# Where the context's expert gathers run: rates of the background queue and 64 gathers of v in a hybrid backbone kernel

## The chip, the core and the metric

The kernel runs on one core of a Trainium2 chip. The metric is the device time of one execution in microseconds (us). A core has five engines with queues of their own: PE (TensorE, matrix products), DVE (VectorE), ACT (ScalarE), POOL (GpSimd, which here only issues indirect DMAs, the gathers) and SP (SyncE, which issues the plain DMAs). PEld is the weight load of PE. Each queue runs in the order in which its instructions stand, and waits for others by semaphores.

## What is computed

Two layers over 512 latent tokens and 256 context tokens of width 1024. A layer has a mixer and an expert stage (PEER):

```
p = h @ w_in[l]                    # one projection feeds four branches and their gates
ml, state = mlstm(p, state)        # two directions, state carried from the context's scan
z = [ml, gmlp(p), conv(p), fnet(p)]
y = sum(sigmoid(p_gate[i]) * (z[i] @ w_branch[i]) for i in range(4))
x = x + mod[2] * (y @ w_out)
# PEER: 8 heads x 16 experts of 16384 for each token
s = einsum('nhpk,pek->nhpe', hb @ w_q, keys); e, g = top16(s)
a = gelu(einsum('nhkd,nd->nhk', u_tab[e], hb)) * g
x = x + mod[5] * einsum('nhk,nhkd->nd', a, v_tab[e])
```

The context goes through PEER in layer 0 alone, and its result is needed first in layer 1's mixer.

## The kernel before

All activations lie transposed, channels on partitions. Products in fp32 accuracy are made of three passes with a high and a low half of each operand: `wload` (L298 to L302) loads 512 KB of weights on SP's queue, ACT makes the high half `wh`, DVE the low half `wl`, and PE runs 24 matmuls (`mm3`, L312). The programs' helper then calls `tick(5.1)`.

For PEER the kernel treats tokens in two ways. Three blocks of 128 latent tokens are computed densely: all experts' products `s` are formed in 128 "s-blocks" (some, 76 in layer 0 and 80 in layer 1, beside the routing, the rest in `dense`), and multiplied by the routing weights (`weights_dense`, L1079 to L1112) and by v (`acc`, L1191). The fourth latent block and the 256 context tokens fetch their experts' rows instead: one gather is an indirect DMA of 128 rows, 512 KB (`rows`, L907). A block of 128 tokens needs 128 gathers of u and 128 of v. For the latents' block each u gather is consumed by one DVE instruction (L938) and each v gather by another (L956). For the context (`gather_ctx`) there are four halves of 64 tokens, with 64 gathers of u and 64 of v each: a u gather is consumed by one DVE instruction of 1024 columns (L1017), two v gathers, a pair, by four matmuls of PE with 32 columns of weights (L1051).

Buffers: the context's u gathers in layer 0's mixer use the tile `ug` (3 buffers), v gathers the tile `gat` (5 buffers, of which one holds the diagonal `dg` for 16 pairs). POOL's queue issues gathers in order, each as soon as its buffer is free.

The gathers are fed into the program by a queue, `rows_bg`: each `tick(us)` of the foreground adds `us * rate` to a credit, and each unit of credit lets one gather be written into the program (a scheduler may then still move instructions a little on each engine). So the rates set beside which work the gathers stand. In layer 0 the queue holds, in this order: u of half 0 (64), then v of half 0 and u of half 1 in turns (128), then u of half 2 (64). The deferred ones are `gens`: v of half 1 and v of half 2 go into the routing of the latents' PEER (`first` of `peer_lat`, at 0.6 credit each and a rate of 0.4), u and v of half 3 into layer 1's mixer. In the routing the gathers of u for the latents' block follow, once that of `first` is done, and what is then left of them goes into `dense`, spread evenly over its 128 steps.

The stages of layer 0 from there on: the context's routing (L1378, up to 584 us), the latents' mLSTM (L1386), `conv` (L1387), four merges with `gmlp` and `fnet` between them (L1393 to L1397), `w_out` (L1402), and the latents' PEER (L1406): norm, 16 steps of the query product (the q steps), the rest of the routing, `dense`. Layer 1 has the same stages of the latents' PEER, but with no context gathers in them.

Of the kernel before, what the change touches and what calls it, by code (L numbers as in the profile page):

```python
# [37 lines left out]
NEG = -1.0e30  # L38
NCAND = 50
STARTS = [0, 16, 24, 29, 33, 36, 38, 40]  # L40
RATE = 0.75
RATE_A = 1.0
ML_TICK = 8.0
P_RATE = 0.28
P0 = (0.4, 0.35, 76)
# [16 lines left out]
def build(nc, tc, I, out):  # L62
# [119 lines left out]
    rows_bg, s_bg, ada_bg, conv_bg = (Background() for _ in range(4))  # L182
# [1136 lines left out]
    with psum_pool(mm=3, sm=3, acc=2):  # L1319
        mod, mod2 = (mk(pl, [128, 48, 2], F32, "modT") for _ in range(2))  # L1320
        C = layer_consts(0)
        mp_cm, mp = open_pool("mp", "left")
        with spool("cxa", 1) as cxa:
            cx_cm, cx = open_pool("cx", "left")
            use_bufs(cx, cx, CTX)
            third = lambda l, g, m: ada_bg.add(ada(l, g, m, cxa, NADA, ("acc", "acc")), 8, 2.0)
            ag = [third(0, g, mod) for g in range(3)]
            ada_bg.finish(ag[0])
            mixer_consts(0, C, cm)
            use_bufs(cx, cx, CTX)  # L1330
            hc = norm_mod(xc, CTX, mod, 1, C["norm1_g"], 0)
            ada_bg.rate = ADA_RATE
            side[0] = "right"
            zc, state = mlstm(0, C, hc, CTX, None, True, True, "zm")
            side[0] = "left"
            def lat_norm():
                use_bufs(pb, cx, SEQ)
                x_first(mp)
                nc.gpsimd.dma_start(xd.rearrange("(k p) t -> p k t", p=128), xl[0])
                hl.extend(norm_mod(xl[0], SEQ, mod, 0, C["norm1_g"], 0))  # L1340
                use_bufs(cx, cx, CTX)

            hl = []
            ctx_merge(0, C, mod, xc, hc, lambda: zc, lat_norm, lambda: ada_bg.finish(ag[2]))
            cx_cm.__exit__(None, None, None)
            cx_cm, cx = open_pool("cx", "left")
            use_bufs(cx, cx, CTX)
            ada_bg.rate = ADA_RATE2
            for g in range(3):
                third(1, g, mod2)  # L1350
            hc = norm_mod(xc, CTX, mod, 1, C["norm2_g"], 3, True)
            nc.gpsimd.dma_start(xcd.rearrange("(k p) t -> p k t", p=128), xc)
            close_right(xc_cm)
            pg_cm, pg[0] = right_pool("pg")
            pu_cm, pu[0] = right_pool("pu")
            hnd = mk(pd, [3, 128, D], F32, "hnd", 1)
            ond = mk(pd, [4, 128, 512], F32, "ond", 1)
            gens = []

            def start(b, i12, gw):  # L1360
                ua, va, ub, vb = gather_ctx(0, hc, b, i12, gw, hnd, ond)
                if b == 0:
                    rows_bg.add(ua(), 64)
                    rows_bg.add(weave(va(), 64, ub(), 64), 128)
                    rows_bg.rate = RATE_A
                    gens.append(vb)
                else:
                    rows_bg.add(ua(), 64)
                    gens.extend([va, ub, vb])

            big = mk(mp, [128, 5136], F32, "x")
            proj = (big[:, 0:2048].rearrange("p (j t) -> p j t", j=4),
                    big[:, 2048:3088].rearrange("p (c h d) -> p c h d", c=4, h=4),
                    big[:, 3088:4112].rearrange("p (c d) -> p c d", c=4),
                    big[:, 4112:5136].rearrange("p (c d) -> p c d", c=4))
            s_bg.add(mlstm_steps(0, C, hl, SEQ, *proj), 13)
            s_bg.rate, s_rate[0] = 0.0, P_RATE
            routing(0, C, hc, CTX, None, start)  # L1378
            s_bg.finish()
            ada_bg.finish()  # L1380
            after[0] = None
            cx_cm.__exit__(None, None, None)
        rows_bg.rate = RATE
        use_bufs(pb, None, SEQ)
        cv_cm, cv = right_pool("cv")
        zl_, _ = mlstm(0, C, hl, SEQ, state, True, False, None, proj)  # L1386
        end = conv(0, C, hl, SEQ, cv)  # L1387
        mp_cm.__exit__(None, None, None)
        zq_cm, zpool[0] = open_pool("zq", "left")
        zl_ = mlstm_z(zl_, SEQ, "zm")  # L1390
        with spool("ym", 1) as ym:
            y = mk(ym, [128, KT, SEQ], F32, "y")
            merge_one(0, 0, True, y, zl_, hl, SEQ)  # L1393
            for i in (1, 3):
                with spool("zb", 1) as zpool[0]:
                    merge_one(0, i, False, y, branch(i, 0, C, hl, SEQ), hl, SEQ)
            merge_one(0, 2, False, y, end(), hl, SEQ)  # L1397
            close_right(cv_cm)
            yp = y_parts(y, SEQ)
        zq_cm.__exit__(None, None, None)  # L1400
        cm_cm.__exit__(None, None, None)
        px = lat_tail(0, yp, mod)  # L1402
        rows_bg.finish()
        close_right(pu_cm)
        pu[0] = None
    peer_lat(0, C, mod, [g() for g in gens[:2]])  # L1406
    rows_bg.add(gens[2](), 64)


    mod_c, mod = mod, mod2  # L1410
    with psum_pool(mm=3, sm=3, acc=2):
# [8 lines left out]
        with spool("zx", 1) as zx:  # L1420
            xc = mk(zx, [128, KT, CTX], F32, "zm")
            nc.sync.dma_start(xc, xcd.rearrange("(k p) t -> p k t", p=128))
            rows_bg.add(gens[3](), 64)
            use_bufs(pb, zx, SEQ)
            with spool("ym", 1) as ym:
                y = mk(ym, [128, KT, SEQ], F32, "y")
                end = conv(1, C, hl, SEQ, zx)
                zs = {i: branch(i, 1, C, hl, SEQ, "z%d" % i) for i in (3, 1)}
                merge_one(1, 3, True, y, zs[3], hl, SEQ)
                merge_one(1, 1, False, y, zs[1], hl, SEQ)  # L1430
                z2 = end()
                with spool("mp", 1) as mp:
                    proj = mlstm_proj(1, C, hl, SEQ, True, mp)
                    rows_bg.finish()
                    for i in range(4):
                        add_ctx(xc, i, ond[i], mod_c)
                    close_right(pg_cm)
                    side[0] = "right"
                    use_bufs(zx, None, CTX)
                    hc = norm_mod(xc, CTX, mod, 1, C["norm1_g"], 0, tags=("z3", "z1"))  # L1440
                    _, state = mlstm(1, C, hc, CTX, None, False, True)
                    use_bufs(pb, zx, SEQ)
                    zl_, _ = mlstm(1, C, hl, SEQ, state, True, False, "zm", proj)
                    merge_one(1, 2, False, y, z2, hl, SEQ)
                    merge_one(1, 0, False, y, zl_, hl, SEQ, (zx, "ca", "ch", "cz", "z3"))
                    side[0] = "left"
                yp = y_parts(y, SEQ)
# [116 lines left out]
```

## Time and profile before

| | us |
|---|---|
| three runs | 4582.52, 4598.94, 4600.25; median 4598.94 |
| the profiled execution | 4583.28 |
| its span, first to last instruction | 4581.5 |
| mean granted clock of PE | 0.956 of full speed |
| PE busy, share of the span | 92% |
| DVE busy | 72% |
| POOL busy | 28% |

The profiled execution is close to the fastest of the three runs, and 15.7 us below their median. Busy time of PE is counted with matmuls that overlap, so a stretch in which PE is busy nearly throughout is a stretch in which PE bounds the work only if nothing waits for it.

### The profile page before, as it was taken

The numbers are of one execution on the slowest core, as the hardware profiler recorded it, in microseconds if no ns is written. First come the engines' busy times: TensorE is split into PE (matmuls) and PEld (weight loads), VectorE is DVE, ScalarE is ACT, GpSimd is POOL, SyncE is SP. The second block draws the span as 40 slices with busy tenths as digits, with TensorE's granted clock in tenths as the row PEclk, the third lists the DMA queues.
The fourth block names the chain that finished last, engine by engine and source line by source line (L and its number), as shares of the span: only waits on it lengthen the run. The fifth ranks groups of instructions, "written<-read, shape, count | busy, mean of one in ns | idle before, by whom it ended". The sixth has DMA issues, their size and how long they took to land.

```text
span 4581.5 us, 61303 instructions
## 1 busy us (share of the span) xinstructions
PE 4230.8 (92%) x22364; PEld 3452.1 (75%) x22364; DVE 3320.1 (72%) x6764; ACT 1628.5 (36%) x2314; POOL 1293.2 (28%) x1061
## 2 busy tenths in 40 slices
PE   7899769988999999999999888989999999999998
PEld 4796545556667799788888764577789998888887
DVE  3764878757578497777778686365699997777775
ACT  4441222223224355333333331243335554333333
POOL 0000246643243331233334244200012322232231
PEclk9999859989999999999999999989999999999999
DMA  7546768986577896999999787622348889898994
GB/s 279 198 151 218 260 216 315 328 291 219 185 265 249 311 341 244 346 333 323 331 323 327 250 281 252 204 65 74 92 141 299 318 291 322 304 310 312 321 312 165
DMA packets 417342, 1187.42 MB, mean 259 GB/s; under 512 B 39440, under 2 KB 142608, under 8 KB 413968
## 3 DMA queue, kind: packets, MB, share of 16 engines
q1 hardware_dynamic: 260992, 631.52, 40.4%
q0 software_dynamic: 150928, 549.52, 33.7%
q8 instruction: 176, 2.88, 0.2%
q10 hardware_dynamic: 5120, 2.47, 0.2%
q14 instruction: 126, 1.03, 0.1%
HBM read 1092.40 MB, written 90.96 MB: 258 GB/s over the span
## 4 chain that ended last, share of the span: by engine, by line
PE 42%; issue 19%; DMA 16%; DVE 10%; POOL 6%; ACT 1%; POOLq 0%; SPq 0%; DVEq 0%; ACTq 0%
PE mm L312 13%; PE s L312 10%; PE acc L1191 10%; POOL gat L907 4%; DMA gsr<-sp 4%; DMA gat<-in_peer_v,ev 3%; DMA gat<-in_peer_v,eu 2%; PE sm L1110 2%; POOL ug L907 2%; DMA vr<-in_peer_v 2%; DMA ug<-in_peer_u,hu 2%; DVE wl L293 1%; DVE gat L938 1%; DMA gat<-in_peer_u,eu 1%; PE mm L809 1%
## 5 line engine op out<-in xcount | busy, mean ns | idle before, releaser
L292 ACT CAST wh<-wr 128x1024 fp32r<-128x1024 f32 x498 | 521.7, 1048 | 1224.9 <-PE mm L312 696.7
L293 DVE TENSOR_TENSOR wl<-wr,wh 128x1024 fp32r<-128x1024 f32 x498 | 607.7, 1221 | 348.6 <-ACT wh L292 344.1
L312 PE MATMUL s<-hh,wh 128*128 128x384 f32 x2048 | 701.6, 343 | 2.5 <-ACT gs L1134 2.5
L312 PE MATMUL s<-hh,wl 128*128 128x384 f32 x2048 | 694.4, 339 | 4.7 <-DVE wl L293 4.7
L312 PE MATMUL s<-hl,wh 128*128 128x384 f32 x2048 | 693.5, 339 | 0.0
L907 POOL DMA_INDIRECT gat<-in_peer_u,eu x256 | 335.0, 1309 | 1245.3 <-PE s L312 463.0
L312 PE MATMUL mm<-hh,wl 128*128 128x512 f32 (+1 forms) x1552 | 589.1, 381 | 35.3 <-DVE wl L293 35.2
L312 PE MATMUL mm<-hh,wh 128*128 128x512 f32 (+1 forms) x1552 | 592.4, 384 | 26.0 <-ACT wh L292 7.8
L1191 PE MATMUL acc<-vh,al 128*128 128x512 f32 x1536 | 602.0, 392 | 14.4 <-DVE al L293 14.2
L1191 PE MATMUL acc<-vh,ah 128*128 128x512 f32 x1536 | 599.7, 392 | 9.5 <-ACT vh L292 6.8
L1191 PE MATMUL acc<-vl,ah 128*128 128x512 f32 x1536 | 600.5, 391 | 7.9 <-DVE vl L293 7.9
L312 PE MATMUL mm<-hl,wh 128*128 128x512 f32 (+1 forms) x1552 | 585.3, 378 | 3.8 <-DVE hl L293 2.3
L907 POOL DMA_INDIRECT gat<-in_peer_v,eu x256 | 323.1, 1262 | 652.0 <-PE acc L1191 511.3
L292 ACT CAST vh<-vr 128x1024 fp32r<-128x1024 f32 x256 | 268.8, 1050 | 526.9 <-DMA vr<-in_peer_v 505.5
L907 POOL DMA_INDIRECT gat<-in_peer_v,ev x256 | 302.4, 1181 | 472.9 <-PE acc L1051 349.5
L312 PEld LDWEIGHTS s<-hh,wh 128*128 128x128 f32 x2048 | 386.2, 189 | 28.1 <-issue 13.8
L312 PEld LDWEIGHTS mm<-hh,wh 128*128 128x128 f32 x1552 | 305.8, 198 | 130.1 <-issue 43.3
L312 PEld LDWEIGHTS mm<-hh,wl 128*128 128x128 f32 x1552 | 305.7, 197 | 115.3 <-DVE wl L293 43.3
L312 PEld LDWEIGHTS s<-hh,wl 128*128 128x128 f32 x2048 | 385.7, 188 | 5.7 <-DVE wl L293 5.7
L312 PEld LDWEIGHTS s<-hl,wh 128*128 128x128 f32 x2048 | 386.2, 189 | 4.4 <-issue 0.8
L956 DVE SCALAR_TENSOR_TENSOR hn<-gat,a,hn 128x1024 f32<-128x1024 f32 x254 | 325.4, 1281 | 85.0 <-DMA gat<-in_peer_v,eu 84.4
L293 DVE TENSOR_TENSOR vl<-vr,vh 128x1024 fp32r<-128x1024 f32 x256 | 312.9, 1223 | 87.8 <-ACT vh L292 86.7
(378 smaller groups left out, 6995.6 us busy)
## 6 DMA issues: line engine op xcount, KB each, us to landing
wr<-in_peer_uT SPq DMA_DIRECT2D x256, 512.0 KB, 5.3
vr<-in_peer_v SPq DMA_DIRECT2D x256, 512.0 KB, 6.0
wr<-in_w_inT SPq DMA_DIRECT2D x134, 512.0 KB, 4.6
wada<-in_w_adaT SPq DMA_DIRECT2D x96, 512.0 KB, 4.6
gd<-gt SPq DMA_DIRECT2D x24, 2048.0 KB, 7.6
gr<-gd SPq DMA_DIRECT2D x64, 768.0 KB, 8.7
sp<-gs SPq DMA_DIRECT2D x78, 384.0 KB, 4.8
gsr<-sp SPq DMA_DIRECT2D x78, 384.0 KB, 6.3
```

The lines of the kernel that those rows point to most:

```text
L292: S.copy(hi, src)
L293: V.tensor_tensor(lo, src, hi, ALU.subtract)
L312: PE.matmul(ps, w[k][a], x[k][b], start=first and k == 0 and i == 0, stop=last and k == n - 1 and i == 2)
L809: after[0] = PE.matmul(ps[:, :T], w[:, k, :], h[k][0], start=k == 0, stop=k == KT - 1)
L907: d = G.indirect_dma_start(out=t, out_offset=None, in_=tab, in_offset=bass.IndirectOffsetOnAxis(ap=ix, axis=0))
L938: V.scalar_tensor_tensor(t, t, 1.0, hn, op0=ALU.mult, op1=ALU.mult, accum_out=a[:, i:i + 1])
L956: V.scalar_tensor_tensor(on, t, a[:, i:i + 1], on, op0=ALU.mult, op1=ALU.add)
L1110: PE.matmul(ps[:, 128 * i:128 * i + 128], o2[:, i].rearrange("p a b -> p (a b)"), o1[:, i, :], start=True, stop=True)
L1191: mm = PE.matmul(acc[b][half], a[p][:, ts], v[q][:, ds], start=done == 0 and n == 0, stop=done == 127 and n == 2)
```

## The change

Three rates replace two: 0.7 instead of 1.0 in the context's routing, 0.45 instead of 0.75 in the latents' mLSTM, 0.9 instead of 0.75 from `conv` to `w_out`. And v of half 1, so far the first of the deferred generators, is put into the queue of layer 0's mixer, behind u of half 2; the latents' routing then begins with v of half 2 alone.

```
-RATE = 0.75
-RATE_A = 1.0
+RATE_A, RATE_ML, RATE = 0.7, 0.45, 0.9
...
                 else:
                     rows_bg.add(ua(), 64)
+                    rows_bg.add(gens.pop(0)(), 64)
                     gens.extend([va, ub, vb])
...
-        rows_bg.rate = RATE
+        rows_bg.rate = RATE_ML
         use_bufs(pb, None, SEQ)
         cv_cm, cv = right_pool("cv")
         zl_, _ = mlstm(0, C, hl, SEQ, state, True, False, None, proj)
+        rows_bg.rate = RATE
         end = conv(0, C, hl, SEQ, cv)
...
-    peer_lat(0, C, mod, [g() for g in gens[:2]])
-    rows_bg.add(gens[2](), 64)
+    peer_lat(0, C, mod, [gens[0]()])
+    rows_bg.add(gens[1](), 64)
...
-            rows_bg.add(gens[3](), 64)
+            rows_bg.add(gens[2](), 64)
```

After the change the kernel's line numbers are lower by one up to `start` (L1050 is L1051 of before).

DVE's queue in the latents' mLSTM, before. One iteration (one head and direction) goes from one product `e` (L570) to the next; `ug` are the context's u rows:

```order
L570 TENSOR_TENSOR e_5469<-e_5469,qks_5458 128x512
L1017 SCALAR_TENSOR_TENSOR ug_5508,ha_889_4614<-ug_5508,hn_4624 128x1024
L537 TENSOR_TENSOR nt_5518<-x_3583,col_5313 128x260
L561 COPY cs_5551<-cst_764 64x65
L1017 SCALAR_TENSOR_TENSOR ug_5511,ha_889_4614<-ug_5511,hn_4624 128x1024
L566 SCALAR_TENSOR_TENSOR cs_5551<-cs_5551,dec_5347,sm_5520 64x65
L1017 SCALAR_TENSOR_TENSOR ug_5514,ha_889_4614<-ug_5514,hn_4624 128x1024
L566 SCALAR_TENSOR_TENSOR cs_5551<-cs_5551,dec_5347,sm_5520 64x65
L548 TENSOR_TENSOR e_5527<-masks_216,sm_5525 128x512
```

The same place after the change (L569 is the product `e`):

```order
L569 TENSOR_TENSOR e_5424<-e_5424,qks_5413 128x512
L588 TENSOR_TENSOR dn_5443<-dn_5443,col_5283 128x4
L565 SCALAR_TENSOR_TENSOR cs_5449<-cs_5449,dec_5317,sm_5417 64x65
L589 RECIPROCAL dn_5443<-dn_5443 128x4
L536 TENSOR_TENSOR nt_5467<-x_3583,col_5283 128x260
L594 TENSOR_TENSOR nt_5435<-nt_5435,dn_5443 128x4x64
L560 COPY cs_5500<-cst_764 64x65
L1016 SCALAR_TENSOR_TENSOR ug_5514,ha_889_4614<-ug_5514,hn_4624 128x1024
L595 TENSOR_TENSOR hacc_5319<-hacc_5319,nt_5435 128x4x64
```

Counted over the queue: from the first to the last of the eight products `e`, 31 u rows stood on DVE's queue and 14 stand there now; ahead of the first, 37 and now 33. What is missing stands between the last product and the first merge's evacuation (9 before, 21 now).

PE's queue at the end of `w_out` and the norm of the latents' PEER (`ones` are its channel sums), before:

```order
L312 MATMUL mm_8836<-hh_8567,wh_8832 128x512
L312 MATMUL mm_8836<-hl_8568,wh_8832 128x512
L312 MATMUL mm_8836<-hh_8567,wl_8833 128x512
L1051 MATMUL acc_8995<-gat_8996,gat_9066 32x512
L318 MATMUL mm_8887<-tA_8888,ones_77 32x128
L318 MATMUL mm_8887<-tA_8894,ones_77 32x128
L1051 MATMUL acc_8995<-gat_8998,gat_9066 32x512
```

After the change, in the midst of `w_out`; `acc` with `gat` are the context's v pairs of half 1:

```order
L311 MATMUL mm_8796<-hh_8641,wh_8776 128x512
L1050 MATMUL acc_8394<-gat_8542,gat_8411 32x512
L311 MATMUL mm_8796<-hl_8642,wh_8776 128x512
L311 MATMUL mm_8796<-hh_8641,wl_8777 128x512
L311 MATMUL mm_8796<-hh_8641,wh_8776 128x512
L311 MATMUL mm_8796<-hl_8642,wh_8776 128x512
L1050 MATMUL acc_8394<-gat_8586,gat_8411 32x512
L1050 MATMUL acc_8394<-gat_8542,gat_8411 32x512
L1050 MATMUL acc_8394<-gat_8586,gat_8411 32x512
```

And at its end, after the last of `w_out`'s 192 matmuls:

```order
L311 MATMUL mm_9063<-hl_8642,wh_9043 128x512
L311 MATMUL mm_9063<-hh_8641,wl_9044 128x512
L1050 MATMUL acc_8394<-gat_8897,gat_8840 32x512
L1050 MATMUL acc_8394<-gat_8899,gat_8840 32x512
L1050 MATMUL acc_8394<-gat_8897,gat_8840 32x512
L1050 MATMUL acc_8394<-gat_8899,gat_8840 32x512
L1050 MATMUL acc_8394<-gat_8939,gat_8840 32x512
```

Before, no v pair stood among `w_out`'s matmuls. Now 2 pairs stand at the end of the last merge, 18 among `w_out`'s matmuls and 12 in one piece behind them, ahead of the norm.

PE's queue in the rest of the routing, before: between the s-blocks (`s`) and the routing weights (`sm`) stand pairs of v of half 2.

```order
L1110 MATMUL sm_11226<-rstd_11222,tA_11224 128x128 x4
L1051 MATMUL acc_10505<-gat_11116,gat_10551 32x512
L1051 MATMUL acc_10505<-gat_11171,gat_10551 32x512
L1051 MATMUL acc_10505<-gat_11116,gat_10551 32x512
L1051 MATMUL acc_10505<-gat_11171,gat_10551 32x512
L1110 MATMUL sm_11242<-rstd_11238,tA_11240 128x128 x4
L312 MATMUL s_11257<-hh_8944,wh_11253 128x384
```

Behind the q steps there were 37 such pairs and are 5 now, none of them among the routing weights. In norm and q steps together there are 27 pairs as before. With the routing's credit free sooner, 81 of the latents' u gathers stand in the routing instead of 45, and 47 instead of 83 in `dense` (128 of v there as before): the numbers that layer 1 has in both kernels.

## Rows read from the trace of the kernel before

**Rows 1.** Windows of layer 0, from the context's routing to `dense`.

```profile
core 0: us, PE busy (x) PEld busy (x) DVE busy (x) ACT busy (x) POOL busy (x), PEclk, DMA share, GB/s
...
584.00:710.00 126.00, 82.03 (x377) 60.53 (x375) 95.70 (x217) 28.37 (x63) 52.55 (x48) 0.65 0.64 205
710.00:741.00 31.00, 25.95 (x94) 11.92 (x93) 26.67 (x47) 8.31 (x13) 23.38 (x19) 0.89 0.95 346
741.00:983.00 242.00, 217.23 (x938) 133.02 (x938) 170.50 (x276) 56.49 (x78) 140.39 (x120) 0.94 0.91 326
983.00:1130.00 147.00, 122.50 (x522) 95.11 (x520) 104.40 (x160) 41.00 (x54) 61.70 (x51) 0.91 0.72 243
1130.00:1177.00 47.00, 45.75 (x194) 35.89 (x194) 22.10 (x27) 13.03 (x18) 0.00 (x0) 1.00 0.48 146
1177.00:1336.00 159.00, 154.05 (x802) 95.07 (x801) 107.69 (x533) 45.35 (x66) 59.17 (x54) 0.99 0.66 225
1336.00:1850.00 514.00, 486.98 (x3021) 436.93 (x3019) 390.47 (x884) 228.33 (x281) 155.68 (x124) 0.98 0.80 288
1850.00:2612.00 762.00, 742.14 (x3509) 640.54 (x3509) 584.84 (x738) 257.56 (x362) 266.57 (x212) 0.99 0.91 318
```

**Rows 2.** Windows of layer 1: a merge, q steps, rest of the routing, dense.

```profile
2819.00:2938.00 119.00, 106.03 (x480) 52.31 (x473) 32.30 (x40) 19.25 (x25) 47.11 (x48) 0.97 0.75 256
...
3256.00:3375.00 119.00, 113.37 (x588) 91.65 (x581) 105.29 (x531) 44.35 (x65) 0.00 (x0) 0.96 0.23 71
3375.00:3830.00 455.00, 444.80 (x2794) 439.88 (x2792) 431.13 (x959) 232.96 (x285) 117.11 (x84) 0.99 0.80 287
3830.00:4564.00 734.00, 722.28 (x3413) 624.77 (x3413) 536.70 (x656) 249.85 (x351) 215.13 (x172) 1.00 0.86 296
```

**Rows 3.** DVE's timeline, the product e of four iterations: start us, us.

```profile
645.23 0.74 DVE L570 TENSOR_TENSOR e<-e,qks 128x512 f32<-128x512 f32 x1
...
658.21 0.66 DVE L570 TENSOR_TENSOR e<-e,qks 128x512 f32<-128x512 f32 x1
...
702.97 0.69 DVE L570 TENSOR_TENSOR e<-e,qks 128x512 f32<-128x512 f32 x1
...
710.51 0.69 DVE L570 TENSOR_TENSOR e<-e,qks 128x512 f32<-128x512 f32 x1
```

**Rows 4.** POOL's timeline: first and last of 22 u gathers; one behind a half's change.

```profile
639.63 0.94 POOL L907 DMA_INDIRECT ug<-in_peer_u,hu  x1 [4.94 <-DVE ug L1017]
...
688.48 1.21 POOL L907 DMA_INDIRECT ug<-in_peer_u,hu  x1 [1.87 <-DVE dn L590]
...
700.95 0.94 POOL L907 DMA_INDIRECT ug<-in_peer_u,hu  x1 [7.94 <-DVE ug L1017]
```

**Rows 5.** Waits in 2819:2938: us in total, times, longest.

```profile
POOL gat L907 <- PE acc L1051: 62.2, 20, 6.0
```

**Rows 6.** POOL's timeline in layer 0's norm, the first, second and fifth of v.

```profile
1180.21 0.94 POOL L907 DMA_INDIRECT gat<-in_peer_v,ev  x1 [70.55 <-PE mm L318]
1181.45 0.94 POOL L907 DMA_INDIRECT gat<-in_peer_v,ev  x1 [0.30 <-PE acc L1051]
...
1189.56 0.94 POOL L907 DMA_INDIRECT gat<-in_peer_v,ev  x1 [4.69 <-PE acc L1051]
```

**Rows 7.** PE's timeline in the same norm: two pairs of v.

```profile
1187.52 1.76 PE L1051 MATMUL acc<-gat,gat 128*32 128x512 f32 x6 [0.27 <-DMA gat<-in_peer_v,ev]
...
1190.30 1.72 PE L1051 MATMUL acc<-gat,gat 128*32 128x512 f32 x8
```

**Rows 8.** Page, part 6, issues: KB each, median us from issue to landing.

```profile
gat<-in_peer_v,ev POOLq DMA_INDIRECT x256, 6.0
...
ug<-in_peer_u,hu POOLq DMA_INDIRECT x192, 5.7
```

**Rows 9.** PE's groups in 1336:1850: busy us, mean ns.

```profile
L1051 PE MATMUL acc<-gat,gat 128*32 128x512 f32 x296 | 49.6, 635 | 15.4 <-DMA gat<-in_peer_v,ev 15.4
```

**Rows 10.** DVE's group of the context's u rows, `ug`, in the whole span.

```profile
L1017 DVE SCALAR_TENSOR_TENSOR ug<-ug,hn 128x1024 f32<-128x1024 f32 x192 | 233.8, 1221 | 95.6 <-DMA ug<-in_peer_u,hu 88.7 <-DMA hn<-hnd 5.7 <-ACT gat L999 0.6
```

## Prediction

> **What bounds the kernel now.** I read the windows first, stretch by stretch, because the shares over the whole span mix stages with different limits. In layer 0's mLSTM (584 to 710 us) no engine is full: PE is busy 82 of 126 us at a granted clock of 0.65, DVE 96 [rows 1]. There a chain of small steps runs through DVE, and the context's u gathers stand in the same queue. DVE's timeline shows their price: an iteration with six u rows takes 13.0 us (645.23 to 658.21), one with three takes 7.5 (702.97 to 710.51) [rows 3]. From the first merge to the end of `fnet` (741 to 983) the DMA engines are 91% busy at 326 GB/s while POOL issues 120 gathers [rows 1]: 2.02 us each. The last two merges (983 to 1130) have spare DMA time (72%), and `w_out` (1130 to 1177) has no gathers: PE is busy 45.8 of its 47 us [rows 1]. It is PE's, without slack.
>
> In the latents' PEER PE is nearly full again. Here layer 1 is a twin: the same work without the context's gathers. From the last q step to the first `acc` matmul layer 0 takes 514 us, layer 1 455; `dense` takes 762 and 734 [rows 1, 2].
>
> **How fast gathers can go.** A u stream is bound by its three buffers: in the mLSTM 22 issues take 48.9 us from first to last, 2.33 us each [rows 4], with a landing of 5.7 us [rows 8]. A stream of v alone is bound by its round trip: in layer 1's merge from 2819 to 2938 us 48 v gathers take 119 us [rows 2], 2.48 each or 4.96 a pair, and POOL waits 62 us for PE to free a buffer [rows 5]. A row of layer 0's norm shows the same with hardly any other work: four gathers were issued, and the fifth came 9.35 us behind the first [rows 6], 4.7 us a pair.
>
> The Trainium skill, "DMA: Bandwidth & Descriptors", section "Anatomy of one DMA — SWDGE (gpsimd) path", gives about 2.0 us and the bytes at 436 GB/s for a DMA issued from GpSimd. By it a gather of 512 KB would land in 3.2 us and a pair's period would shrink by 2.8 us; the trace has 6.0 us as the median landing of these gathers [rows 8], so I go by the row.
>
> **The change, part by part.** The base is the profiled execution, 4583.3 us (span 4581.5).
>
> 1. Fewer u rows in the routing and the mLSTM. Seventeen fewer stand between the first and the last product `e`. The floor is DVE's own time, 1.22 us a row [rows 10], so 21 us; the slope of the two iterations, 5.5 us for three rows [rows 3], gives 31. I take 25, since one iteration in the trace with three rows is already near 7.5 us. Four fewer ahead of the loop are worth 5 us (1.22) to 9 (2.33); I take 7. Together −32.
>
> 2. They come back. Twenty-one u rows instead of nine now stand between the loop and the first merge's evacuation, and DVE's queue holds the weights' low halves behind them. At 2.33 us they take 49 us where that stretch took 31 [rows 1]: +18. The change from half 0 to half 1, which reloads `hn` and left POOL waiting 7.9 us [rows 4], falls into this stretch as well: +7. So +25 of the 32 is lost again.
>
> 3. First merge to `fnet`: 66 u and 56 v rows before, 60 and 60 now, on a stretch that DMA bounds. 0.
>
> 4. The last two merges. Fifteen of half 2's u rows stood ahead of `fnet`'s end and none does now; all 64 fall on 983 to 1130. At 2.33 us, with three of them in flight, 142 us: just inside the 147 that PE needs anyway. Two v pairs at the end (1.3 us each, 49.6 us for 37 pairs [rows 9]) and some in-order waits: +5. If the stream went no faster than here before, 49 rows in 134 us or 2.7 each (estimated from the order's count and this window), +25.
>
> 5. `w_out`. Half 1's 64 v gathers, 128 matmuls, two diagonals on POOL and DVE, the copy and the store move here whole. They stand behind half 2 in POOL's queue, so they can't start earlier, and only five buffers let them run ahead. Eighteen pairs among `w_out`'s matmuls at 4.96 us make 89 us; twelve in one piece behind them at 4.7 make 56. The norm's matmuls stand behind these on PE, and the q steps and all DVE work of the routing wait for the norm. 145 us in place of 47: **+98**. SP's queue isn't touched: its loads only come less densely.
>
> 6. Norm and q steps: 27 pairs before and after. 0.
>
> 7. The rest of the routing and `dense`. The PE order there becomes layer 1's, with five v pairs in front. Layer 1 needs 455 + 734 = 1189 us, layer 0 now 1276 [rows 1, 2]: −87, and five pairs cost 7. The four s-blocks that layer 0 has more in `dense` and fewer in the routing cancel. **−80**. Two sources lie in it: 32 pairs less on PE (43 us by the same 1.34) [rows 9] and 36 u gathers less in a `dense` at 91% DMA.
>
> Sum: −32 + 25 + 0 + 5 + 98 + 0 − 80 = +16 us, or 4599 beside the profiled 4583.3. The median of the runs shown, 4598.9, lies 15.7 above that execution; on its footing the time is **4615 us**. The routing's relief is real, but `w_out` can hide little of what it is given.
>
> **The rivals.**
>
> *PE's clock falls in `w_out`* (slower). PE would be waiting for gathers between its matmuls. In the mLSTM, with PE busy 82 of 126 us, the granted clock was 0.65 [rows 1], and in the norm six matmuls of a pair took 1.76 us [rows 7] where 37 pairs averaged 1.34 each. At half clock `w_out`'s 192 matmuls need 94 us and 18 pairs 48 to 65, so 142 to 159 in place of 89: about +60 more, 4675 us. Against it: in the v-only merge PE was busy 106 of 119 us and kept 0.97 [rows 2], and here it would be busy 47 and 18 times 1.3 to 1.6, some 73 of 89. It decides where the granted clock of the stretch falls under 0.75. The Trainium skill, "TensorE: Matmul & The Clock Gate", section "HAM oscillation — how this bites in real kernels", says that a loop in which TensorE keeps waiting for DMA swings between its two rates (1.2 and 2.4 GHz); no row here shows it for a stretch of this kind.
>
> *The u stream falls behind in the last merges* (slower): part 4 at its other end, +20 more, 4635 us. For it: the rates rise while the three buffers don't. Against it: the mLSTM had 2.33 us [rows 4] even with DVE and DMA both in use.
>
> *The v gathers flow as fast as POOL issues them* (faster). Issues follow each other in 1.24 us [rows 6]. Then `w_out` is bound by PE alone, 47 + 18 × 1.34 = 71 us, and the tail by issue, 12 × 2.48 = 30: 101 instead of 145, −44, so 4571 us. For it: `w_out` leaves the DMA engines half idle (48%) [rows 1]. Against it: the norm's 9.35 us for four gathers came with DMA at its lightest. It decides at a pair period under 4.0 us. By the page on DMA named above this is what would happen.
>
> *`dense` is DMA's, not PE's* (no change to faster). Thirty-six gathers of 512 KB at 318 GB/s are 59 us, where part 7 counts only 28 in `dense` (762 − 734). −31 more: 4584 us. Against it: `dense` of layer 1 moves less and still takes 734, with PE busy 722 [rows 2].
>
> *Nothing moves.* The rates could only shift credit; the queues show that it does move, so no chance of its own.
>
> **How the numbers follow.** Half a per cent, 23 us, is about what a measurement of this kernel tells from no change. My forecast, with its own range of −10 to +40 us (4589 to 4639), has a chance of 0.50, 0.32 within that bound and 0.18 above it. The clock rival has 0.09 and the u rival 0.13, both slower by nearly all of it (0.20, and 0.02 within). The fast rival has 0.16: 0.12 faster, 0.04 within. The `dense` rival has 0.12: 0.06 faster, 0.05 within, 0.01 slower. Together faster 0.18, same 0.43, slower 0.39. The unknown costs reach from −20 (part 5 at POOL's pace with part 1 at its slope) to +75; leaving a tenth at each end, 4575 to 4665 us.
>
> **What would show it.** The first merge's evacuation near 734 us (741 before) and the last merge's end near 1128; the norm's first matmul near 1275 instead of 1177; in `w_out` POOL waiting for PE's `acc` and PE for the gathers' landing, with a pair every 4.7 to 5 us; norm and q steps near 159 us; then 455 to 465 us to the first `acc` of `dense`, and `dense` near 734 to 750. Wrong is the forecast if the norm starts before 1240 or after 1310, or if the rest of the routing keeps more than 490 us, which would mean that neither PE nor DVE was what it waited for. Layer 1 should keep its times to a few us.

## The result, and the profile after

| | before | after |
|---|---|---|
| median, us | 4596.73 (4 runs, 4582.52 to 4600.25) | 4644.0 (4 runs, 4635.19 to 4654.4) |
| profiled execution, us | 4583.28 | 4650.03 |
| span, us | 4581.5 | 4648.3 |

The ratio is 1.011, 95% interval 1.009 to 1.013: the change makes the kernel slower by 1.1%. The two spans differ by 66.8 us, and the stages below add up to that. The medians differ by 47 us: the profiled execution of before lies 13 us under its median and that of after 6 us above, so some 20 of the 66.8 us belong to these two executions and not to the change.

The windows of after, cut at its own stages; they answer to [rows 1, 2]. Columns as there.

```profile
core 0: us, PE busy (x) PEld busy (x) DVE busy (x) ACT busy (x) POOL busy (x), PEclk, DMA share, GB/s
584.00:682.00 98.00, 66.10 (x288) 50.85 (x288) 64.44 (x162) 16.96 (x47) 30.41 (x25) 0.53 0.37 123
682.00:746.00 64.00, 35.39 (x130) 22.74 (x131) 45.91 (x76) 12.99 (x19) 29.24 (x25) 0.71 0.74 243
746.00:986.00 240.00, 222.06 (x944) 128.71 (x943) 161.93 (x263) 55.89 (x76) 140.46 (x120) 0.97 0.92 330
986.00:1165.00 179.00, 132.76 (x554) 100.02 (x553) 123.00 (x189) 43.17 (x58) 84.59 (x69) 0.87 0.74 246
1165.00:1265.00 100.00, 90.54 (x337) 40.14 (x335) 20.69 (x26) 11.48 (x15) 37.10 (x39) 0.95 0.77 266
1265.00:1313.00 48.00, 28.83 (x99) 3.94 (x100) 2.05 (x3) 2.17 (x3) 20.73 (x23) 0.86 0.79 261
1313.00:1473.00 160.00, 155.57 (x811) 96.77 (x803) 105.89 (x531) 44.58 (x65) 64.73 (x59) 0.98 0.66 233
1473.00:1929.00 456.00, 441.34 (x2760) 429.50 (x2758) 427.02 (x954) 228.66 (x280) 115.75 (x93) 0.99 0.82 293
1929.00:2678.00 749.00, 739.52 (x3506) 640.70 (x3509) 544.96 (x666) 257.74 (x361) 224.77 (x176) 0.99 0.86 298
2678.00:4630.00 1952.00, 1853.12 (x9625) 1563.98 (x9616) 1451.10 (x2845) 729.46 (x1006) 494.60 (x389) 0.97 0.69 241
```

Read it against the stages of before. The mLSTM's loop is over at 682 instead of 710, but the 31 us to the first merge's evacuation are now 64. The last two merges take 179 us instead of 147 with the DMA engines no busier (0.74). `w_out` takes 100 instead of 47, and 48 us of nothing but v pairs follow. Routing and `dense` (1313 to 2678) take 1365 instead of 1435; layer 1 is as it was.

DVE's timeline of after, the first and the last u row of half 2 (64 rows in all):

```profile
987.97 1.22 DVE L1016 SCALAR_TENSOR_TENSOR ug<-ug,hn 128x1024 f32<-128x1024 f32 x1
...
1158.41 1.23 DVE L1016 SCALAR_TENSOR_TENSOR ug<-ug,hn 128x1024 f32<-128x1024 f32 x1 [1.72 <-DMA ug<-in_peer_u,hu]
```

Sixty-three steps in 170.4 us are 2.71 us a row. The waits of after from 986 to 1165 us say what a row waits for (us in total, times, longest):

```profile
POOL ug L906 <- DVE ug L1016: 71.5, 42, 3.9
DVE ug L1016 <- DMA ug<-in_peer_u,hu: 50.2, 33, 3.8
```

POOL waits for DVE to free a buffer, DVE for the gather to land: three buffers going round. v of half 1 stands behind half 2's u in the queue that feeds the program, but on POOL the first four of its gathers went out early, among the u gathers. POOL's timeline of after in the last two merges and in `w_out`:

```profile
989.54 1.62 POOL L906 DMA_INDIRECT gat<-in_peer_v,ev  x1 [0.30 <-issue]
...
1016.52 0.93 POOL L906 DMA_INDIRECT gat<-in_peer_v,ev  x1 [0.30 <-issue]
...
1151.93 1.68 POOL L906 DMA_INDIRECT ug<-in_peer_u,hu  x1 [0.78 <-DVE ug L1016]
1163.18 0.93 POOL L906 DMA_INDIRECT gat<-in_peer_v,ev  x1 [9.58 <-PE acc L1050]
...
1173.82 0.94 POOL L906 DMA_INDIRECT gat<-in_peer_v,ev  x1 [5.92 <-PE acc L1050]
...
1178.49 0.94 POOL L906 DMA_INDIRECT gat<-in_peer_v,ev  x1 [2.49 <-PE acc L1050]
...
1183.17 0.94 POOL L906 DMA_INDIRECT gat<-in_peer_v,ev  x1 [2.50 <-PE acc L1050]
```

The four early gathers and the diagonal fill the tile's five buffers by 1033 us. The fifth gather waits for the first pair's matmuls, and these stand on PE behind the step that closes half 2's u rows. PE's timeline of after at that place:

```profile
1161.57 0.33 PE L1023 MATMUL acc<-ident,ha 64*64 64x64 f32 x4 [1.64 <-DVE ha L1020]
1161.83 1.92 PE L1050 MATMUL acc<-gat,gat 128*32 128x512 f32 x16
```

So the other sixty gathers of half 1 start at 1163 us, once half 2's u is done. From then on POOL waits for PE to free buffers before nearly every pair; ten of the 17 steps from pair to pair in `w_out` are 4.67 or 4.68 us (1173.82, 1178.49, 1183.17), and the mean is 5.3. That alone does not say whether PE waits for the gathers or the gathers for PE. The waits of after from 1165 to 1313 us, for POOL, and then PE's waits for a landing, first from 1165 to 1265 and then from 1265 to 1313 us:

```profile
POOL gat L906 <- PE acc L1050: 73.7, 28, 5.9
```

```profile
PE acc L1050 <- DMA gat<-in_peer_v,ev: 9.5, 7, 3.4
```

```profile
PE acc L1050 <- DMA gat<-in_peer_v,ev: 19.2, 20, 2.0
```

In `w_out` PE waited for gathers for 9.5 of 100 us, behind it for 19 of 48. What else takes PE's time in `w_out` stands in its timeline (`acc` are the v pairs, `mm` the matmuls of `w_out`; a matmul of a pair has two records, so a pair has eight):

```profile
1179.97 1.05 PE L1050 MATMUL acc<-gat,gat 128*32 128x512 f32 x2
1180.95 0.50 PE L311 MATMUL mm<-hh,wl 128*128 128x512 f32 x1
...
1181.84 1.06 PE L1050 MATMUL acc<-gat,gat 128*32 128x512 f32 x6
...
1184.65 1.05 PE L1050 MATMUL acc<-gat,gat 128*32 128x512 f32 x2
```

Each of these pairs is cut into two pieces, one matmul and three, with matmuls of `w_out` between them. A piece of one takes as long as a piece of three. From 1179.97 to 1184.65 us PE ran ten matmuls of `w_out`, at 0.23 us each, and two pieces; that leaves 1.17 us a piece, or 2.34 us a pair. So the step of 4.68 us is PE's own work here. Sixteen of the 18 pairs stand cut like this.

The landing of the v gathers in after's DMA view (median us from issue), which answers to [rows 8]:

```profile
gat<-in_peer_v,ev POOLq DMA_INDIRECT x256, 5.8
```

### The profile page after: what moved, and what is told of

It reads as the page before. It is cut to its first block, busy times and chain, and to the rows that moved or that the text cites. A ratio compares the mean times of both kernels' runs of the same rounds, so it can differ in the third digit from the quotient of the medians.

```text
span 4648.3 us, 61281 instructions
## 1 busy us (share of the span) xinstructions
PE 4272.2 (92%) x22364; PEld 3458.5 (74%) x22364; DVE 3317.4 (71%) x6764; ACT 1629.6 (35%) x2313; POOL 1288.1 (28%) x1061
## 4 chain that ended last, share of the span: by engine, by line
PE 54%; issue 16%; DMA 10%; DVE 9%; POOL 5%; ACT 1%; ACTq 0%; POOLq 0%; DVEq 0%; SPq 0%
PE acc L1190 17%; PE s L311 14%; PE mm L311 14%; DMA gat<-in_peer_v,ev 3%; POOL gat L906 3%; POOL ug L906 2%; PE sm L1109 2%; DVE wl L292 2%; PE acc L1050 2%; DMA ug<-in_peer_u,hu 1%; DMA gsr<-sp 1%; PE mm L808 1%; DMA vr<-in_peer_v 1%; DMA gat<-in_peer_u,eu 1%; DVE gat L937 1%
## 5 line engine op out<-in xcount | busy, mean ns | idle before, releaser
L906 POOL DMA_INDIRECT gat<-in_peer_v,ev x256 | 280.3, 1095 | 352.4 <-PE acc L1050 297.6
```

The source lines that it names most:

```text
L906: d = G.indirect_dma_start(out=t, out_offset=None, in_=tab, in_offset=bass.IndirectOffsetOnAxis(ap=ix, axis=0))
```

## The experiments

Each run's ratio is against the kernel before on the same chip. The stage ends are the last or first matmuls of one profiled execution each, in us from the span's start.

| kernel | last u row | last merge ends | norm starts | layer 0's dense ends | ratio, 95% interval |
|---|---|---|---|---|---|
| before | 1114.5 | 1130.0 | 1178.1 | 2611.2 | |
| after | 1158.4 | 1165.1 | 1312.6 | 2677.4 | 1.011 (1.009 to 1.013) |
| e1 rates alone | 1143.6 | 1149.6 | 1198.3 | 2631.4 | 1.0049 (1.0032 to 1.0066) |
| e2 move alone | 1114.3 | 1136.0 | 1260.4 | 2626.0 | 1.0016 (1.0004 to 1.0028) |
| e3 v of half 1 left out | 1147.1 | 1153.4 | 1203.8 | 2562.9 | 0.9877 (0.9861 to 0.9892) |
| e4 four u buffers | 1086.5 | 1129.7 | 1238.3 | 2601.8 | 0.9948 (0.9934 to 0.9962) |
| e5 v in the u buffers | 1144.4 | 1156.3 | 1269.4 | 2638.3 | 1.0025 (1.0012 to 1.0039) |
| e6 before, four u buffers | 1073.9 | 1097.0 | 1143.5 | 2589.0 | 0.9927 (0.9907 to 0.9948) |
| e7 both of e4 and e5 | 1089.9 | 1128.6 | 1205.4 | 2565.8 | 0.9893 (0.9875 to 0.9911) |
| e8 e7 at a rate of 1.1 | 1087.2 | 1193.9 | 1260.7 | 2621.1 | 1.001 (0.9995 to 1.0026) |
| e9 e7 at the old rates | 1076.7 | 1102.3 | 1196.3 | 2557.1 | 0.9865 (0.9843 to 0.9886) |
| e10 e7 at rates between | 1069.7 | 1088.2 | 1183.5 | 2546.9 | 0.9831 (0.9808 to 0.9854) |
| e11 v of half 1 in layer 1 | 1063.2 | 1085.1 | 1131.6 | 2496.1 | 0.9988 (0.9971 to 1.0006) |
| e12 one index tile | 1148.2 | 1157.4 | 1299.1 | 2657.3 | 1.0074 (1.0059 to 1.009) |

**The theory**: v of half 1 in `w_out` costs more than the routing gives back, and half 2's u rows, all pushed into the last merges, go at the pace of three buffers. **The rivals**: v of half 1 is what slows the last merges; or the DMA engines, not the buffers, set the paces. A third, that PE's own time for the pairs sets the pace in `w_out`, had no run of its own; the traces decide it.

**e1, the rates alone.** In the kernel before:

```
-RATE = 0.75
-RATE_A = 1.0
+RATE_A, RATE_ML, RATE = 0.7, 0.45, 0.9
...
+        rows_bg.rate = RATE_ML
         use_bufs(pb, None, SEQ)
...
+        rows_bg.rate = RATE
         end = conv(0, C, hl, SEQ, cv)
```

> The three new rates alone; v of half 1 stays ahead of the latents' routing as before. Theory (half 2's 64 u rows all fall on the last two merges and go at 2.7 us each): the last merge ends near 1165 us as in the changed kernel (1130 before), w_out takes 47 us, the norm starts near 1212, the rest of the routing 514, dense 762: span about 35 us over before, ratio 1.0075. Rival (the 35 us in the last merges come from v of half 1 standing behind them in POOL's and PE's queues): the last merge ends within 5 us of 1135 and the ratio is within 0.2% of 1.

The last merge ends 19.6 us later than before, w_out takes 47. Windows and waits (986 to 1150 us) of e1:

```profile
985.00:1046.00 61.00, 52.71 (x230) 40.98 (x228) 44.57 (x67) 14.43 (x19) 32.95 (x28) 0.97 0.85 290
1046.00:1150.00 104.00, 67.12 (x285) 50.43 (x277) 73.54 (x115) 25.89 (x35) 43.97 (x36) 0.85 0.74 246
```

```profile
POOL ug L906 <- DVE ug L1016: 70.2, 44, 4.0
...
DVE ug L1016 <- DMA ug<-in_peer_u,hu: 43.6, 33, 3.1
```

With no v of half 1 near, the same waits stand in the same place: the first rival falls as the main cause. The expectation was 35, the trace says 20. From the end of `fnet` to the end of the last merge e1 takes 171 us and e3, without v of half 1, 170, where before takes 147: 22 to 24 are the rates' price. With v of half 1 in its place (after, e5, e12) the same stretch takes 177 to 179 us. So the first rival is right for some 8 us: the early gathers, the first diagonal and the pairs at the end of the merge stand in it. The rest of after's 35 is where the stretch begins, 986.5 us against 983 before and 978 to 984 in e1, e3, e5 and e12; no run explains that.

**e2, the move alone**, at the old rates:

```
-RATE_A, RATE_ML, RATE = 0.7, 0.45, 0.9
+RATE_A, RATE_ML, RATE = 1.0, 0.75, 0.75
```

> The move alone, at the old rates: 10 of half 1's v gathers stand in the last merge, 31 among w_out's matmuls, 23 behind them in one piece. Theory: the mLSTM and the first merges keep the times of before (last merge's end 1130 to 1137), the 27 pairs left take 15.5 x 4.96 + 11.5 x 4.1 = 124 us in place of w_out's 47 (+77), routing and dense give 70 back: about +10 to +15 us, ratio 1.003. Rival (v of half 1 slows the last merges): the last merge ends near 1165, +40 to +45 us, ratio 1.01.

The last merge ends 6 us later than before, and 124.4 us pass from there to the norm (expected: 124). Windows of e2, `w_out` and what is behind it:

```profile
1136.00:1209.00 73.00, 70.78 (x313) 38.86 (x312) 22.03 (x27) 12.43 (x17) 31.29 (x31) 1.00 0.85 298
1209.00:1260.00 51.00, 31.41 (x100) 4.02 (x99) 2.05 (x3) 2.14 (x3) 21.88 (x23) 0.80 0.75 254
```

After needs 147.5 us there. One reason is when u of half 2 is done, 1114 or 1158 us: in e2 the fifth gather of v went out at 1119, and more pairs were through before `w_out`. Another is the order on PE: in e2 14 pieces of pairs stand among `w_out`'s matmuls, in after 33. The expected 124 came from buffer round trips, and that it fits is partly luck: PE waited 2 of the 73 us of e2's `w_out`. So the two halves of the change cost more together (1.1%) than apart (0.5 and 0.2).

**e3, v of half 1 left out**, from the changed kernel:

```
+                if i == 1:
+                    on = mk(pg[0], [128, 512], F32, "gat", GB)
+                    G.memset(on, 0.0)
+                    nc.gpsimd.dma_start(ond[i], on)
+                    yield
+                    return
                 for p in range(32 + VLAG):
...
-                    rows_bg.add(gens.pop(0)(), 64)
+                    rows_bg.add(gens.pop(0)(), 1)
```

> The changed kernel with v of half 1 left out of the computation: its 64 gathers and 128 matmuls are gone, zeros are stored in place of its sum. It prices the rates and the relief without the exposed gathers. Theory: last merge's end near 1160, w_out 47 to 50 us, norm near 1210, then routing and dense 70 us shorter than before: 35 us faster than before, ratio 0.992. Rival (the last merges are slowed by v of half 1): last merge's end near 1130 and 65 to 70 us faster, ratio 0.985. Second rival (routing and dense were relieved by something other than the moved gathers, and depend on the late norm): they return to 1276 us and the ratio is above 1.0.

The last merge still ends 23 us late, and norm to the end of `dense` takes 1359.1 us (1433.0 before): the relief of 74 is that of the missing gathers with their matmuls and doesn't depend on a late norm. The second rival falls. The ratio, 0.9877, lies between the theory's 0.992 and the first rival's 0.985. In the whole table the stretch is 1358 to 1369 us wherever v of half 1 is gone from it, and 1433 to 1446 wherever it is there.

**e4 and e12, four u buffers.** The fourth is paid for with one of two index tiles of the routing; e12 has the second line alone.

```
-UB, ULAG, VLAG = 3, 2, 1
+UB, ULAG, VLAG = 4, 2, 1
...
-            i12 = mk(pg[0], [128, 2, 128], F32, "i12", 2)
+            i12 = mk(pg[0], [128, 2, 128], F32, "i12", 1)
```

> The changed kernel with four buffers for the u rows in place of three (a second buffer of the routing's index tile is given up for the space). Theory (the round trip over three buffers binds the u rows of the last merges): the period there falls from 2.7 to about 2.0 us, the last merge ends between 1125 and 1140 in place of 1165, everything behind it keeps its lengths: 25 to 35 us under the changed kernel, ratio 1.004. Rival (the rows wait for their place in DVE's in-order queue, or for the weights that share the DMA): the last merge still ends near 1160, ratio 1.011.

> The changed kernel with the routing's index tile in one buffer in place of two and nothing else: the other half of the edit with which the fourth u buffer was paid for. Theory (the fourth buffer alone made that gain): same as the changed kernel, norm near 1300 to 1313, ratio 1.009 to 1.012. Rival (the single index tile changes the order in the routing and is part of the gain): ratio under 1.005.

e12 lies below what was expected (1.0074; norm at 1299.1), so up to 0.4% of the gain may be the index tile's or the chip's. The fourth buffer is worth the rest: norm at 1238.3 instead of 1299.1, 1.3% of the time. DVE's timeline of e4, first and last u row of a stretch with 58, and its windows from the last merge on:

```profile
959.38 1.23 DVE L1016 SCALAR_TENSOR_TENSOR ug<-ug,hn 128x1024 f32<-128x1024 f32 x1 [1.85 <-DMA ug<-in_peer_u,hu]
...
1086.45 1.23 DVE L1016 SCALAR_TENSOR_TENSOR ug<-ug,hn 128x1024 f32<-128x1024 f32 x1 [0.41 <-DMA ug<-in_peer_u,hu]
```

```profile
1021.00:1130.00 109.00, 81.97 (x338) 52.37 (x340) 62.60 (x96) 26.58 (x34) 51.01 (x45) 0.86 0.80 273
1130.00:1221.00 91.00, 85.70 (x345) 39.23 (x338) 21.76 (x28) 13.58 (x19) 37.66 (x39) 0.98 0.83 284
1221.00:1238.00 17.00, 9.98 (x34) 1.24 (x32) 1.81 (x2) 0.65 (x1) 7.45 (x8) 0.90 0.84 283
```

A row takes 2.23 us instead of 2.71. The gain was larger than expected, since the first merge ends 32 us earlier too (776.3; 808.8 in e12), and since the fifth gather of v goes out at 1093 us. In e12 the u rows still take 2.64 us each, so the pace is the fourth buffer's and not the index tile's.

**e6, the kernel before with four u buffers** (the same two lines).

> The kernel before (old rates, v of half 1 in the latents' routing) with four u buffers. Theory (three buffers hold up the u rows, and DVE's queue behind them, in the mLSTM and the merges whatever the rates): the last merge ends near 1100 in place of 1130, ratio 0.993. Rival (the fourth buffer helps only where the change crowds the u rows together): within 0.2% of 1. If it is 0.993, the change is worth nothing with four buffers either (0.9948 with it).

It came out as the theory said, 0.9927. Three buffers held up the kernel before as well; with four, e6 (0.9927) and e4 (0.9948) show the change worth nothing still. In e6 a u row of the last merges takes 2.30 us, in before 2.67.

**e5 and e7, v in the u buffers**, with three and with four of them:

```
-                            ts[p].append(rows(v_tab, ev[:, tok:tok + 1]))
+                            ts[p].append(rows(v_tab, ev[:, tok:tok + 1], i == 1 and q == 0))
```

> The changed kernel, three u buffers; the first gather of each pair of half 1's v goes into the u rows' buffers, which are free by then, so that three pairs can be under way where two were. Theory (the pair's period in w_out is a round trip over few buffers): w_out takes 71 to 82 us in place of 100, the twelve pairs behind it 30 to 36 in place of 47, the norm starts between 1265 and 1285 in place of 1312.6: 30 to 45 us under the changed kernel, ratio 1.001 to 1.004. Rival (the landing under a DMA share of 0.77 to 0.84 binds the pair, whatever the buffers): the period stays above 4.3 us, the norm starts near 1305, ratio 1.01.

> The changed kernel with four u buffers, and the first gather of each pair of half 1's v in them. Theory: the gains add: last merge's end near 1130, w_out 71 to 80 us in place of 91, the norm near 1205 to 1212 in place of 1238: 25 to 33 us under the run with four u buffers alone, ratio 0.988. Rival (DMA, at a share of 0.83 in that run, binds w_out): the norm starts after 1230, ratio 0.994.

Windows of e5, then of e7, `w_out` and what is behind it:

```profile
1157.00:1245.00 88.00, 87.53 (x350) 38.64 (x352) 20.66 (x26) 12.10 (x16) 39.24 (x41) 1.00 0.90 318
1245.00:1269.00 24.00, 16.79 (x65) 2.48 (x64) 2.05 (x3) 1.48 (x2) 12.93 (x13) 0.79 0.90 323
```

```profile
1130.00:1197.00 67.00, 66.38 (x340) 39.69 (x336) 21.06 (x26) 11.64 (x15) 41.30 (x39) 1.00 1.00 386
1197.00:1205.00 8.00, 5.80 (x34) 0.98 (x26) 1.63 (x3) 1.02 (x2) 3.52 (x3) 1.00 0.92 335
```

Both ratios are as expected, but not for the reason given. In e5 `w_out` itself gained less (88 us, expected 71 to 82) and the tail more (24, expected 30 to 36). PE is busy 87.5 of these 88 us and waits 0.7 for landings, and nine of 19 steps from pair to pair are 4.68 us still: among `w_out`'s matmuls stand 19 pairs in 35 pieces, nearly all of them cut. So in `w_out` the buffers were worth the 12 us that it got shorter, and more behind it; the rest is PE's own time. In e7 16 pairs stand there, whole, two or three together, in seven pieces. PE's timeline of e7 around two pairs (the 16 records of the two lie between):

```profile
1144.34 0.40 PE L311 MATMUL mm<-hh,wl 128*128 128x512 f32 x1
1144.66 0.62 PE L1050 MATMUL acc<-ug,gat 128*32 128x512 f32 x1
...
1145.99 0.59 PE L1050 MATMUL acc<-gat,gat 128*32 128x512 f32 x1
1146.52 0.50 PE L311 MATMUL mm<-hh,wh 128*128 128x512 f32 x1
```

From the matmul before the two pairs to the one behind them are 2.18 us instead of 0.23, so a pair costs about 1 us instead of 2.34, and `w_out` takes 67 us. What makes the scheduler cut pairs in one kernel and not in another isn't shown, and no run changed that alone. PE and the DMA engines are both full in e7's `w_out`, so which of them bounds it isn't shown either; the rival of the DMA engines could be right only there.

**e8, a higher rate** (e7 with RATE 1.1).

> As the run before it, at a rate of 1.1 in place of 0.9 from conv on, so that all of v of half 1 stands ahead of w_out, 50 of its gathers in the last merge. Theory (the stretch from the first merge on is DMA's at 2.0 us a gather, so a higher rate only shifts work): the last merge ends some 45 us later, w_out takes 47 us, the norm starts within 10 us of the run before, ratio 0.987 to 0.990. Rival (more rows in DVE's queue delay the merges' own steps again): the norm starts 20 us later or more, ratio 0.993 or above.

The rival's time came, the norm starts 55 us later. But its reason is not what makes the last merge long: the u rows are done at the same time (1087 and 1090), and still that merge takes 1054 to 1194. Windows of the last merge of e8, then of e7, and a wait of e8 from 1054 to 1195 us:

```profile
1054.00:1195.00 141.00, 116.00 (x456) 53.19 (x456) 49.90 (x73) 26.45 (x36) 75.78 (x69) 0.88 0.84 287
```

```profile
1027.00:1130.00 103.00, 79.07 (x350) 53.35 (x352) 62.13 (x95) 27.59 (x37) 55.15 (x49) 0.85 0.86 301
```

```profile
ACT wh L291 <- PE mm L311: 69.8, 8, 12.5
```

PE is idle for 25 us in the one and 24 in the other, and busy 37 us longer in e8. There the pairs of the last merge stand in 41 pieces, most of them cut pairs, in e7 in five pieces of two whole pairs. Counted in the traces, these pieces add 47 us on PE in e8 and 9 in e7. So PE's queue delays the merge, and the high halves `wh` wait for PE rather than PE for them. The merge also begins 27 us later than in e7 (1054 and 1027); whether rows in DVE's queue cost that isn't shown.

**e9 and e10, other rates in e7**: (1.0, 0.75, 0.75), and (0.85, 0.6, 0.8).

> The run with four u buffers and v of half 1 in them, at the old rates (1.0, 0.75, 0.75). Theory (the new rates push half 2's u rows into the last merges, which costs more there than they free in the routing and the mLSTM): the last merge ends near 1103 us in place of 1129, the 27 pairs left take 80 to 85 us, the norm starts between 1180 and 1192 in place of 1205: 13 to 25 us under that run, ratio 0.985. Rival (with four buffers the new rates are worth their 17 us at the first merge): the norm starts at 1205 or later, ratio 0.989 or above.

> The same with rates between the old and the new (0.85, 0.6, 0.8). By the theory of the run before it half 2's u rows stand in the last merges as with the new rates (31 of them in the last one), so it lies between the two: the norm near 1195, ratio 0.987. Rival (there is a best rate in the middle): the norm before 1180, ratio under 0.985.

Windows of e10, `w_out` and what is behind it:

```profile
1090.00:1152.00 62.00, 61.82 (x311) 38.64 (x312) 20.44 (x26) 10.99 (x14) 34.68 (x33) 1.00 0.99 371
1152.00:1183.00 31.00, 23.63 (x98) 3.57 (x90) 1.97 (x3) 1.27 (x2) 18.52 (x19) 0.89 0.95 362
```

The old rates are a little better than the new (0.9865 and 0.9893, with intervals that just overlap; the norm is 4 us later than expected), and the middle ones best. Fewer u rows then stand in the mLSTM than at the old rates (first merge's end 787.1, with 801.6 in e9), and they are still done by 1070. The ratio is the rival's; the norm, 1183.5, lies between its 1180 and the theory's 1195. e10, 4518.46 us in the median, beats both kernels.

**e11, v of half 1 in layer 1's mixer**, old rates, four u buffers, and the lines

```
-    peer_lat(0, C, mod, [gens[0]()])
-    rows_bg.add(gens[1](), 64)
+    peer_lat(0, C, mod, [gens[1]()])
+    rows_bg.add(weave(gens[2](), 64, gens[0](), 64), 128)
```

with `gens[3]` behind them and RATE1 at 1.6.

> Old rates, four u buffers, and v of half 1 not in layer 0's mixer but in layer 1's, woven with u of half 3 at a rate of 1.6. It prices another place. The mixer of layer 0 is that of the kernel before with four buffers (norm near 1143), the routing and dense of layer 0 give their 69 us back, and 176 gathers in place of 112 stand on layer 1's first 326 us: 2.0 us each would add 26 us there, 2.48 (a v stream over five buffers) 110. Theory (buffers, not the place, set the price): 2.3 or more each, 80 to 110 us, ratio 0.995 to 1.002. Rival (w_out and the tail were the wrong place, PE and DMA have idle time in layer 1): 25 to 40 us, ratio 0.984 to 0.987.

Layer 0 gives 69 us back against before, and from the end of its `dense` to layer 1's norm 756.8 us pass instead of 644.3: +113, where the v stream over five buffers had been priced at 110. Waits of e11 from 2496 to 2852 us:

```profile
POOL gat L906 <- PE acc L1050: 87.3, 28, 8.5
POOL gat L906 <- DVE gat L1016: 81.1, 31, 6.3
```

The theory's ratio came, its reason is not shown. From the end of `dense` to layer 1's norm PE was busy 662 us in e11 and 571 before, so some 90 of the 113 us are PE's work; 32 more pairs stand there, in 62 more pieces.

## Why the prediction was right or wrong

The forecast was 4615 us, a change within half a per cent; 4644 lies in the range, outside the forecast's own 4589 to 4639, and the norm's first matmul at 1312.6 is past the 1310 that the prediction named as its limit. Every part that was forecast to change went in the direction that was forecast, and sizes were off: 51 us between the two profiled executions, some 30 between the medians. Between the stage ends of [rows 1, 3] and of after:

| part | forecast | measured |
|---|---|---|
| 1 routing and mLSTM, to the last product `e` (710.5 to 681.5) | −32 | −29.0 |
| 2 from there to the first merge's evacuation (741.4 to 746.0) | +25 | +33.6 |
| 3 to the end of `fnet` | 0 | −1.2 |
| 4 the last two merges | +5 | +31.7 |
| 5 `w_out` and the pairs behind it | +98 | +99.4 |
| 6 norm and q steps | 0 | +1.8 |
| 7 rest of the routing −57.3, `dense` −12.8 | −80 | −70.1 |
| layer 1 | 0 | +0.6 |
| sum | +16 | +66.8 |

**Part 4** is the term that was most mis-sized: 27 of the 51 us. It took the u rows at 2.33 us each, from the mLSTM [rows 4], and kept 2.7 as a bound. But the same stretch of before had already gone at the bound. DVE's timeline of before, the first and the last of its 50 u rows there:

```profile
983.70 1.22 DVE L1017 SCALAR_TENSOR_TENSOR ug<-ug,hn 128x1024 f32<-128x1024 f32 x1
...
1114.50 1.22 DVE L1017 SCALAR_TENSOR_TENSOR ug<-ug,hn 128x1024 f32<-128x1024 f32 x1
```

That is 2.67 us each, and after went at 2.71. The price should have come from there; the mLSTM, with the DMA engines at 0.64 [rows 1], was the farther row. The rival "the u stream falls behind in the last merges" is what happened, and its price for this part, 25, was right for the rates: the stretch is 22 to 24 us longer in e1 and e3, without v of half 1. The other 8 or so come with v of half 1 (177 to 179 us in after, e5 and e12), which part 4 had at two pairs and some waits, 5.

**Part 2** took the same 2.33 us and came out 9 over the forecast, and the evacuation stood at 746 instead of 734; what the 9 are isn't shown.

**Part 5** is right as a sum by luck: 100 for `w_out` (89 forecast) and 47 behind it (56), and the mechanism holds behind `w_out` alone. The forecast took 4.96 us a pair from layer 1's merge as a round trip through the buffers [rows 5]. But PE was busy 106 of the 119 us of that row [rows 2], and it was busy 90.5 of the 100 in after's `w_out`, where the clock rival's working had 73 of 89. The term that it had wrong is PE's price for a pair, 1.34 us [rows 9]: in `w_out` a pair costs 2.34, since it is cut in two. The order shown ahead of the prediction has the cut, one `acc` matmul and then three. That it looks like the pace of [rows 6], 9.35 us for two pairs, is chance. With hardly any wait, e5's `w_out` still took 88 us. Behind `w_out`, where PE waited 19 of 48 us, the round trip is the bound, at 4.3 us a pair instead of 4.7 (seven steps from 1267.42 to 1297.48).

The **clock rival** falls: granted 0.95 in `w_out`, 0.86 in the tail; it would have needed less than 0.75. The Trainium skill, "TensorE: Matmul & The Clock Gate", section "HAM oscillation — how this bites in real kernels", describes a swing in loops that wait for DMA; this stretch doesn't show one, but PE waited for only 9.5 of its 100 us. The **fast rival** falls as the change stood, since its period of under 4.0 us did not come, neither in `w_out` nor behind it. It was right about what `w_out` could do: in e7, with 16 whole pairs and more buffers, it took 67 us, near the 71 that the rival gave it with 18. What it had wrong was PE's price in `w_out`, and the landing behind it. The Trainium skill, "DMA: Bandwidth & Descriptors", section "Anatomy of one DMA — SWDGE (gpsimd) path", would give 3.2 us for 512 KB, an estimate by its fit; the trace of after has 5.8 in the median, and the measurement decides.

**Part 7** came out at −70: layer 1 as a twin was ten too good, since `dense` kept 749 us against the twin's 734. The `dense` rival falls with it. e3 shows that the relief is that of the moved gathers and their matmuls.

The sign follows from three prices between the profiled executions: the last merge ends 35 us later, `w_out` and the pairs behind it cost 99 more, and 68 come back in routing and `dense`. It turns where `w_out`'s pace does: with four u buffers, v in them as well and the old rates, the moved pairs put the norm 53 us later (e9 against e6, 1196.3 and 1143.5) and free some 85 behind it, 0.9865 against 0.9927.

## What to carry to other kernels

A stream of gathers through k buffers can't go faster than (landing + use) / k, the landing counted from the start of the issue, and both stand in the profile before: for u 5.7 + 1.22 over 3 gives 2.3 us, over 4 it gives 1.7. The mLSTM's rows went at that pace (2.33). Those of the last merges took 2.6 to 2.7 us with three buffers and 2.2 to 2.35 with four (e4, e6, e9), so it is a bound and not a forecast: take the pace from the very stretch that is priced.

Then look at what the pairs cost on the engine that consumes them, in the order in which they will stand: beside the 46 us that `w_out`'s matmuls take alone, 16 whole pairs cost PE 19 us (e7) and 19 pairs, nearly all cut in two, 42 (e5). A wait of POOL for PE doesn't say that the buffers are the bound; PE's own waits do. And look for idle buffers of a neighbour: one more u buffer alone made 0.7% of gain (e6), and with a shared pool and rates between the two sets the same move that cost 1.1% ended at 1.7% of gain (e10).

## What the runs showed of the hardware that was not expected

In e7's `w_out` the 16 DMA engines reached a share of 1.00 at 386 GB/s, with gathers of 512 KB and weight loads mixed, while PE was busy 66.4 of 67 us; the highest in the windows of before was 0.95 at 346 [rows 1]. PE's clock held in `w_out`: it was granted 0.95 in that of after, with 9.5 of 100 us of waits, and 1.00 in that of e5 and e7. It was lower where PE waited more: 0.86 behind `w_out` of after (busy 28.8 of 48 us), 0.80 in e2 (31.4 of 51), and 0.53 in the mLSTM (66 of 98).

The four matmuls of a pair, with 32 columns of weights each, run side by side: in e7 the first four start within 0.02 us (1144.66 to 1144.68). A piece of one such matmul between matmuls of `w_out` held PE as long as a piece of three, 1.05 and 1.06 us in after, and two whole pairs in one piece took 1.95 us in e7.
